# Score products of a differential attention: one mask product per bank ahead of four score products that alternate between two row groups

## Chip, core and metric

The kernel runs on one core of a Trainium2 chip. The metric is the device time of the program in microseconds (us), lower is better. Engines are named TensorE (PE; PEld is its weight load), VectorE (DVE), ScalarE (ACT), GpSimd (POOL) and SyncE (SP, which issues the DMAs here).

## What is computed

One layer of a streaming encoder for 256 tokens of width 2048. A conditioning vector gives shifts, scales and gates; one input projection feeds two groups of heads; an output projection and a gated feed-forward follow. Everything is in f32. One group, `mlstm`, has four heads of a matrix memory. The other, which the change concerns, is a differential attention: eight heads with two softmax maps each over 64 dimensions, and 128-wide values.

```python
def diff_attention(q, k, v, lam):
    # q,k (B,H,2,S,64): two maps; v (B,H,S,128)
    for j in range(S // 128):              # two blocks of 128 queries
        q0 = j * 128; kend = q0 + 128
        s = jnp.einsum('bhmqd,bhmkd->bhmqk', q[:, :, :, q0:kend], k[:, :, :, :kend]) * scale
        allowed = k_chunk[None, :] <= q_chunk[:, None]        # chunks of 64 tokens
        p = jax.nn.softmax(jnp.where(allowed, s, -jnp.inf), axis=-1)
        a = p[:, :, 0] - lam * p[:, :, 1]
        outs.append(jnp.einsum('bhqk,bhkd->bhqd', a, v[:, :, :kend]))
```

A head has four score blocks: query block 0 against 128 keys and query block 1 against 256 keys, for each of the two maps. In each, the last 128 key columns are the diagonal block, in which the first 64 queries may not see the last 64 keys.

## The kernel before

The main stream is a row of 392 "ticks". A tick multiplies 256 rows of a weight matrix, 512 columns wide, with all 256 tokens. Weights and activations are split into a high and a low part (`wh`, `wl` and for instance `hh`, `hl`), so a tick has twelve products of 128x512 into an accumulator `acc` (lines 568 to 570). A weight tile comes by DMA as `r`; ScalarE makes `wh` (line 211), VectorE makes `wl` (line 181). Three raw tiles and four pairs `wh`, `wl` may be alive, and SyncE issues the next load when one comes free.

All other work is written as generators. A planner (`Plan`) places their steps between halves of ticks by estimated costs of each engine and by free banks: four PSUM banks of 128x512 (`misc`, `BANKS = 4`) are shared by this work. The resulting order is fixed when the program is built, and each engine works through its own queue. Among this work are the modulation (`gv`: four products of 128x256 in the four 32-column groups of the array, from tiles `ada`) and the attention.

`attend(h)` handles a head. It takes two banks, `sc[0]` and `sc[1]`, one for each map. The two maps of a head lie on partitions 0 to 63 and 64 to 127 of `qT` and `kT`, so a map's score product uses 64 rows of the array, the lower or the upper ones. The mask is added by a bf16 product of an identity (`identb`) with a mask tile (`bmask`), which uses the whole array. Then VectorE finds negative row maxima (`st`, line 196), POOL scales them, ScalarE takes exp with a sum (`pm`, line 211), which frees the banks, VectorE combines the maps, and TensorE transposes the result (`aT`). `attend_values` multiplies with the values (`po`), and `finish_attention` makes the parts `odh` and `odl` for the output projection. A wait between engines goes by whole tiles: the first maximum of a bank waits for the last product that writes the bank.

Of the kernel before, what the change touches and what calls it, by code (L numbers as in the profile page):

```python
# [12 lines left out]
BF16 = mybir.dt.bfloat16  # L13
# [5 lines left out]
P = 128  # L19
D = 2048  # L20
NEG = -1.0e30
# [57 lines left out]


class Work:
    """Background work in steps; a step follows the one before it by at least a tick."""

    def __init__(self, name, gen, after):
        self.name, self.gen, self.after = name, gen, after
# [2 lines left out]


class Plan:  # L90
    """Interleaves the steps of background work with the ticks of the main matrix products."""

    def __init__(self):
        self.now = 0
# [70 lines left out]
def tile_block(ctx, tc, x, c, pos, par, w_ada, w_in, w_gt, w_out, w_gu, w_dn, out):  # L165
    nc = tc.nc
# [6 lines left out]
    ctx.enter_context(tc.manual_schedule())  # L173
    plan = Plan()

# [1 line left out]
    def fs(ap):  # L177
        return math.prod(ap.shape[1:])

# [15 lines left out]
    def red(o, a, op, negate=False):  # L195
        nc.vector.tensor_reduce(o, a, axis=AX.X, op=op, negate=negate)
        plan.v += fs(a) / 960 + 0.07

    def rec(o, a):
        nc.vector.reciprocal(o, a)  # L200
        plan.v += fs(o) / 120 + 0.07
# [13 lines left out]
    def mm(o, l, r, start, stop, passes=4, **kw):  # L215
        nc.tensor.matmul(o, l, r, start=start, stop=stop, **kw)  # L216
        plan.p += passes * max(fs(r), 64) / 2400

    def tr(o, a):
        nc.tensor.transpose(o, a, ident[:])  # L220
        plan.p += 0.06

    def slab(name, dt=F32):
        return sl.tile([P, 1024], dt, name=name, tag="slab")

    def misc(name):
        return psM.tile([P, 512], F32, name=name, tag="misc")

    def const(shape, name, dt=F32):
        return cp.tile(shape, dt, name=name)  # L230

    def tok(t, i):
        return t[:, i * 512:(i + 1) * 512]

# [1 line left out]
    part = const([P, NPAR - 256], "part")  # L236
    nc.sync.dma_start(part[:], par[:, :NPAR - 256])

    def par_(name):
        o, w = OFF[name]  # L240
        return part[:, o:o + w]
# [14 lines left out]
    for cb in range(4):  # L256
        load_x(cb)

# [1 line left out]
    ones = const([P, P], "ones")  # L260
    nc.gpsimd.memset(ones[:], 1.0)
    ident = const([P, P], "ident")
# [1 line left out]
    identb = const([P, P], "identb", BF16)  # L264
# [9 lines left out]
    for i in range(2):  # L274
# [8 lines left out]
    nc.gpsimd.memset(cmask[:], 0.0)  # L283
    nc.gpsimd.affine_select(out=cmask[:], in_=cmask[:], pattern=[[-1, P]], compare_op=ALU.is_ge,
                            fill=NEG, base=0, channel_multiplier=1)
    bmask = const([P, P], "bmask", BF16)
    nc.gpsimd.memset(bmask[:], 0.0)
    nc.gpsimd.memset(bmask[0:64, 64:128], NEG)
    junk = const([P, 512], "junk", BF16)

    act(scol[:, :, 0], par_("cc"), AF.Silu)
# [3 lines left out]
        mm(pq[:], ones[0:1, :], crow[0:1, q * 512:(q + 1) * 512], True, True)  # L295
        act(tok(silc[q // 2], q % 2), pq[:], AF.Silu)

# [1 line left out]
    items = []  # L299
    for s, t in ((1, 0), (4, 3)):  # L300
        for p in range(8):
# [172 lines left out]
        act(hi[:, q], full, AF.Copy)  # L474
        tt(lo[:, q], full, hi[:, q].bitcast(F32), ALU.subtract)

# [1 line left out]
    ticks = []  # L478

    def visit(accname, first, last, acts, src, name, halves, ready=(), done=None):  # L480
        """halves: list of (kb, half) in the order of K; acts(kb) gives (hi, lo)."""
        for n, (kb, h) in enumerate(halves):
            ticks.append(dict(acc=accname, start=first and n == 0, stop=last and n == len(halves) - 1,
                              act=acts, kb=kb, h=h, src=src, name=name, ready=ready,
                              done=done if n == len(halves) - 1 else None, split=None, mid=None))
# [60 lines left out]
    apart = {}  # L546

    def acc_tile(acc, k):
        """The accumulator of token tile k; those that are drained one by one have tiles of their own."""
        if acc in apart and k == 1:  # L550
            return apart[acc][:]
        return tok(accs[acc], k)
# [17 lines left out]
        nc.tensor.matmul(o, al[:, s], wh[:, r], start=False, stop=t["stop"] and j == 1)  # L570

    def products(i, half):
        """Half of a tick; the two ticks that end a group with "split" go token tile by token tile."""
        t = ticks[i]
        if t["split"] is None:
            for k in range(2):
                product(i, half, k)
        else:
            first = i - t["split"]
            for j in range(2):  # L580
                product(first + half, j, t["split"])
        if half == 1 and t["split"] != 0:
            for n in range(i - (t["split"] or 0), i + 1):
                del wtiles[n]

# [1 line left out]
    ropet = {}  # L587
    wqk = const([P, 1], "wqk")
    lam = const([P, 4], "lam")
# [67 lines left out]
        ts(lam[:, 2:3], lam[:, 2:3], -LAM0, None, ALU.add)  # L657
        ts(subc[:], par_("sub"), 1.0 - LAM0, None, ALU.mult)

# [1 line left out]
    proj = {}  # L661
    gwt = const([P, 16, 16], "gwt", F32R)
    gts = early[:, 768:1024]
    small = slab("small")
# [25 lines left out]
            tt(gts[0:16, :], gts[0:16, :], pg[0:16, 0:256], ALU.add)  # L690
        plan.rel(1)

# [1 line left out]
    sclq = const([P, 2, 16], "sclq")  # L694
    rstk = const([P, 2, 16], "rstk")
    qT, kT = {}, {}
# [55 lines left out]
    def attend(h):  # L752
        g, hh = divmod(h, 4)
        yield 2
        sc = [misc(f"sc{h}_{m}") for m in range(2)]
        blocks = []
        for t in range(2):
            ke = 128 * (t + 1)
            for m in range(2):
                pr = slice(m * 64, m * 64 + 64)  # L760
                o = sc[m][:, t * 128:t * 128 + ke]
                mm(o, qT[g][pr, hh * 256 + t * 128:hh * 256 + t * 128 + 128], kT[g][pr, hh * 256:hh * 256 + ke],
                   True, False)
                mm(o[:, t * 128:], identb[:], bmask[:], False, True, passes=1)
                blocks.append((t, m, o))
        yield 0
        st = sm.tile([P, 2, 8], F32, name=f"st{h}", tag="st", bufs=4)
        for t, m, o in blocks:
            red(st[:, t, m:m + 1], o, ALU.max, negate=True)
        scale = sclq[:, :, h * 2:h * 2 + 2]  # L770
        nc.gpsimd.tensor_tensor(st[:, :, 2:4], st[:, :, 0:2], scale, op=ALU.mult)
        yield 0
        work = slab(f"pm{h}")
        pm = {}
        for t, m, o in blocks:
            ke = 128 * (t + 1)
            a = ((640, 512), (0, 256))[t][m]
            pm[t, m] = work[:, a:a + ke]
            act(pm[t, m], o, AF.Exp, bias=st[:, t, 2 + m:3 + m], scale=scale[:, t, m:m + 1],
                accum=rs0[g][:, hh, t:t + 1] if m == 0 else st[:, t, 4:5])  # L780
        plan.rel(2)
        yield 0
        rec(st[:, :, 5], st[:, :, 4])
        stt(st[:, :, 6], rs0[g][:, hh], lam[:, 2:3], st[:, :, 5], ALU.mult, ALU.mult)
        for t in range(2):
            stt(pm[t, 0], pm[t, 1], st[:, t, 6:7], pm[t, 0], ALU.mult, ALU.add)
        yield 1
        pa = misc(f"aT{h}")
        for t in range(2):
            for s in range(t + 1):  # L790
                tr(pa[:, (t + s) * 128:(t + s + 1) * 128], pm[t, 0][:, s * 128:(s + 1) * 128])
        yield 0
        if h // 2 not in aTs:
            aTs[h // 2] = slab(f"aTs{h // 2}")
        act(aTs[h // 2][:, (h % 2) * 384:(h % 2) * 384 + 384], pa[:, :384], AF.Copy)
        plan.rel(1)
# [45 lines left out]
        plan.rel(2)  # L842
        mixT[2 + g] = (hi, lo)

# [1 line left out]
    cw = par_("cw").rearrange("p (t j) -> p t j", t=8)  # L846
    cbias = par_("cb")
    mT = {}
# [173 lines left out]
        plan.rel(2)  # L1022
        mixT[pair] = (hi, lo)

# [1 line left out]
    def gate_rows(s, rows, name):  # L1026
        yield 0
        modcol(s, 0, 16)
# [37 lines left out]
        return go  # L1066

    def turn(stage, heads):
        """The last products of w_out and the first of w_gate_up go token tile by token tile; this is what lies between."""
        if stage == 0:  # L1070
            residual_half(("wo", 3), rows1, 3, xs[3], 0)
            square_x(1, 3, 0, SQ0)
            finish_rms(1, 0)
            for p in range(2):
                next(heads[p, 0])
        elif stage == 1:
            plan.free -= 2
            for p in range(2):
                next(heads[p, 0])
        elif stage == 2:  # L1080
            residual_half(("wo", 3), rows1, 3, xs[3], 1)
            del accs["wo", 3], apart["wo", 3]
            plan.rel(1)
            next(heads[0, 0], None)
            square_x(1, 3, 1, SQ1)
            next(heads[1, 0], None)
            finish_rms(1, 1)
            for p in range(2):
                next(heads[p, 1])
        elif stage == 3:  # L1090
            plan.free -= 2
            for p in range(2):
                next(heads[p, 1])
        else:
            for p in range(2):
                next(heads[p, 1], None)
            plan.mark("norm2")
# [2 lines left out]
        yield 0  # L1100
        act(junk[:, 0:1], epst[:, 0:1], AF.Sqrt)

# [1 line left out]
    fpart = {}  # L1104
    aT = {}
    out_v = out.rearrange("(t p) (c n) -> c p t n", p=P, n=512)
# [70 lines left out]
        for k in range(2):  # L1177
            ticks[k - 2].update(split=k, mid=fn(k), done=None)

# [1 line left out]
    spans = {}  # L1181

    def pairs(p0, p1):
# [6 lines left out]
    for n, (groups, p0, p1) in enumerate(SWEEPS):  # L1190
        a = len(ticks)
# [4 lines left out]
    a = len(ticks)  # L1196
# [13 lines left out]
    for r, (p0, p1) in enumerate(FSWEEPS):  # L1210
        a = len(ticks)
# [10 lines left out]
    a = len(ticks)  # L1222
# [4 lines left out]
    a = len(ticks)  # L1227
# [6 lines left out]
    spans["dn"] = (a, len(ticks))  # L1234
    group_chunks()

    # how many quarters of w_ada each span of ticks takes: (first tick, last tick, items)
    loads = []

    def load(span, n, margin):  # L1240
# [9 lines left out]
            n += k * min(max(i + 1 - a, 0), b - a) / (b - a)  # L1250
        return min(int(n + 1e-6), len(items))

# [1 line left out]
    plan.t = 3.2  # L1254
    ada_dma(4)
    weights_dma(1)
# [70 lines left out]
        plan.add(f"h1_{p}", make_hT(1, p), [f"ada4_{p}", f"ada3_{p}", "norm2"])  # L1327
    plan.add("rows2", gate_rows(5, rows2, "g2r"), [f"ada5_{p}" for p in range(8)] + ["aT10"])

# [1 line left out]
    pending = []  # L1331
    turning = spans["wo"][1]
    heads = {(p, k): make_h2T(p, k) for p in range(2) for k in range(2)}
# [44 lines left out]


class Lazy:  # L1380
    """A generator that is made when its first step runs; that step needs no bank before it."""

    def __init__(self, fn, *args):
        self.fn, self.args, self.gen, self.asked = fn, args, None, False
# [82 lines left out]
```

## Time and profile before

| | us |
|---|---|
| median of 3 runs | 1253.47 (1249.21 to 1253.92) |
| profiled execution: span, first to last instruction | 1246.5 |
| profiled execution: its own time | not given; only the span is |
| PE busy in the span | 1224.0 (98%) |
| DVE, ACT, POOL busy | 815.9, 587.4, 112.2 |
| mean granted TensorE clock | 0.993 |

The profile shows one execution. A row of a timeline has start, duration, engine, line of the code, operation, output and inputs, shapes and a count; rows of the same kind that follow each other are merged. Matmuls overlap in the array, so TensorE's busy time says little, and distances between starts are what counts. The chain is the work that ended last, followed back from the end: what lies on it sets the time. An f32 score product is recorded as two passes, each with a weight load.

### The profile page before, as it was taken

How to read it: one execution, taken by the hardware profiler on the slowest of the kernel's cores; microseconds unless marked ns; L12 is line 12 of the kernel's file. 1: busy time of each engine (PE TensorE's matmuls, PEld its weight loads, DVE VectorE, ACT ScalarE, POOL GpSimd, SP SyncE). 2: the span in 40 equal slices, each digit the busy share in tenths (PEclk: the TensorE clock that was granted, in tenths of full speed). 3: DMA queues.
4: the chain of work that ended last, by engine and by line, in shares of the span. 5: the costliest groups of instructions: out<-in, count | busy, mean ns of one | idle time of the engine just before them, and what ended most of it. 6: DMA issues, size and time to landing. Idle time of an engine off the chain costs nothing.

```text
span 1246.5 us, 15450 instructions
## 1 busy us (share of the span) xinstructions
PE 1224.0 (98%) x5858; PEld 963.2 (77%) x5858; DVE 815.9 (65%) x1064; ACT 587.4 (47%) x817; POOL 112.2 (9%) x249
## 2 busy tenths in 40 slices
PE   6999999999999999999999999999999999999998
PEld 2667877667778788788888888888888878888886
DVE  2657976557667998777988986555445454545453
ACT  3654444446646644765434454434344443434332
POOL 1010221200302412011100000000000000000000
PEclk9999999989999999999999999999999999999999
DMA  8889997746755989698998856555555545646461
GB/s 332 300 299 349 343 377 282 281 151 249 256 219 194 330 331 353 264 341 302 354 352 332 309 181 218 201 176 200 188 183 197 183 169 195 220 169 223 165 251 54
DMA packets 63260, 313.84 MB, mean 252 GB/s; under 512 B 6993, under 2 KB 7377, under 8 KB 41169
## 3 DMA queue, kind: packets, MB, share of 16 engines
q1 hardware_dynamic: 63186, 312.86, 69.1%
q8 instruction: 46, 0.75, 0.2%
q14 instruction: 28, 0.23, 0.1%
HBM read 310.73 MB, written 2.10 MB: 251 GB/s over the span
## 4 chain that ended last, share of the span: by engine, by line
PE 95%; DMA 2%; DVE 1%; ACT 1%; issue 0%; SPq 0%; POOL 0%; ACTq 0%
PE gv L216 3%; PE sc L216 2%; DMA ada<-in_w_ada_dram 2%; PE acc('dn', 0)_8051 L570 2%; PE acc('dn', 0)_8051 L568 2%; PE acc('dn', 2)_8853 L570 2%; PE acc('dn', 2)_8853 L569 2%; PE acc('dn', 1)_8473 L570 2%; PE acc('dn', 1)_8473 L569 2%; PE acc('dn', 0)_8051 L569 2%; PE acc('dn', 2)_8853 L568 2%; PE acc('dn', 1)_8473 L568 2%; PE apart('dn', 3)_9234 L570 1%; PE apart('dn', 3)_9234 L569 1%; PE acc('dn', 3)_9233 L570 1%; PE acc('dn', 3)_9233 L569 1%
## 5 line engine op out<-in xcount | busy, mean ns | idle before, releaser
L181 DVE TENSOR_TENSOR wl<-r,wh 128x1024 fp32r<-128x1024 f32 x392 | 474.4, 1222 | 252.0 <-ACT wh L211 250.6
L211 ACT ACTIVATE wh<-r 128x1024 fp32r<-128x1024 f32 x392 | 410.3, 1058 | 414.6 <-DMA r<-in_w_gu_dram 64.7
L185 DVE SCALAR_TENSOR_TENSOR ada<-ada,silc 128x1024 f32<-128x1024 f32 x120 | 144.7, 1218 | 0.0
L376 POOL TENSOR_TENSOR modc<-part,gsum 128x2 f32<-128x2 f32 (+1 forms) x34 | 24.5, 722 | 396.5 <-DVE ada L185 277.7
L216 PE MATMUL gv<-ada,early 128*32 128x256 f32 x576 | 47.1, 420 | 4.6 <-DMA ada<-in_w_ada_dram 4.4
L216 PEld LDWEIGHTS gv<-ada,early 128*32 128x32 f32 x576 | 13.3, 112 | 30.5 <-issue 20.7
L568 PE MATMUL acc('dn', 0)_8051<-wh,aTh 128*128 128x512 f32 x88 | 35.9, 408 | 0.0
L378 POOL TENSOR_TENSOR modc<-modc,gsum 128x2 f32<-128x2 f32 (+1 forms) x58 | 30.9, 533 | 46.8 <-DVE ada L185 43.4
L570 PE MATMUL acc('dn', 0)_8051<-wh,aTl 128*128 128x512 f32 x88 | 34.3, 390 | 0.0
L569 PE MATMUL acc('dn', 0)_8051<-wl,aTh 128*128 128x512 f32 x88 | 34.3, 389 | 0.0
L568 PE MATMUL acc('dn', 1)_8473<-wh,aTh 128*128 128x512 f32 x88 | 34.2, 389 | 0.0
L569 PE MATMUL acc('dn', 1)_8473<-wl,aTh 128*128 128x512 f32 x88 | 34.2, 389 | 0.0
L570 PE MATMUL acc('dn', 1)_8473<-wh,aTl 128*128 128x512 f32 x88 | 34.2, 389 | 0.0
L568 PE MATMUL acc('dn', 2)_8853<-wh,aTh 128*128 128x512 f32 x88 | 34.2, 389 | 0.0
L569 PE MATMUL acc('dn', 2)_8853<-wl,aTh 128*128 128x512 f32 x88 | 34.2, 389 | 0.0
L570 PE MATMUL acc('dn', 2)_8853<-wh,aTl 128*128 128x512 f32 x88 | 34.2, 389 | 0.0
L181 DVE TENSOR_TENSOR hl<-hx,hh 128x512 fp32r<-128x512 f32 (+1 forms) x18 | 11.4, 632 | 26.7 <-ACT hh L211 26.6
L211 ACT ACTIVATE hx<-pt,modc,gcol 128x256 f32<-128x256 f32 (+1 forms) x36 | 17.4, 534 | 16.8 <-PE pt L220 11.7
L211 ACT ACTIVATE gr<-gv 128x256 f32<-128x256 f32 x18 | 6.9, 383 | 34.5 <-PE gv L216 34.5
L216 PE MATMUL sc<-kT,qT 64*128 64x128 f32 (+1 forms) x64 | 20.2, 397 | 0.0
L211 ACT ACTIVATE aTh<-at 128x512 fp32r<-128x512 f32 x22 | 11.9, 595 | 17.2 <-PE at L220 17.2
L569 PEld LDWEIGHTS acc('dn', 0)_8051<-wl,aTh 128*128 128x128 f32 x88 | 16.5, 188 | 4.2 <-issue 1.0
(987 smaller groups left out, 3041.6 us busy)
## 6 DMA issues: line engine op xcount, KB each, us to landing
ada<-in_w_ada_dram SPq DMA_DIRECT2D x192, 512.0 KB, 5.6
r<-in_w_gu_dram SPq DMA_DIRECT2D x76, 1024.0 KB, 5.1
r<-in_w_dn_dram SPq DMA_DIRECT2D x44, 1024.0 KB, 4.8
r<-in_w_in_dram SPq DMA_DIRECT2D x36, 1024.0 KB, 7.1
r<-in_w_out_dram SPq DMA_DIRECT2D x16, 1024.0 KB, 7.4
r<-in_w_in_dram SPq DMA_DIRECT2D x24, 512.0 KB, 5.9
r<-in_w_gu_dram SPq DMA_DIRECT2D x24, 512.0 KB, 5.2
x<-in_x_dram SPq DMA_DIRECT2D x4, 512.0 KB, 5.8
```

Of the source, the lines that this page charges most:

```text
L181: nc.vector.tensor_tensor(o, a, b, op=op)
L185: nc.vector.scalar_tensor_tensor(out=o, in0=a, scalar=s, in1=b, op0=op0, op1=op1, accum_out=accum)
L211: nc.scalar.activation(o, a, func, **kw)
L216: nc.tensor.matmul(o, l, r, start=start, stop=stop, **kw)
L376: nc.gpsimd.tensor_tensor(o, parts[0], parts[1], op=ALU.add)
L378: nc.gpsimd.tensor_tensor(o, o, y, op=ALU.add)
L568: nc.tensor.matmul(o, ah[:, s], wh[:, r], start=t["start"] and j == 0, stop=False)
L569: nc.tensor.matmul(o, ah[:, s], wl[:, r], start=False, stop=False)
L570: nc.tensor.matmul(o, al[:, s], wh[:, r], start=False, stop=t["stop"] and j == 1)
```

## The change

The mask tile becomes two copies side by side, 256 columns. For a head, first one mask product goes to each bank, over columns 128 to 383, and opens the accumulation of the bank. Then come four score products: the 256-key block of map 0 and of map 1 into columns 0 to 255, then the 128-key block of map 0 and of map 1 into columns 256 to 383. They add to the mask where there is one and otherwise write. Before, the order was block by block, each score followed by its mask. The planner is told of two passes for a score instead of four.

```diff
-    bmask = const([P, P], "bmask", BF16)
+    bmask = const([P, 2 * P], "bmask", BF16)
     nc.gpsimd.memset(bmask[:], 0.0)
-    nc.gpsimd.memset(bmask[0:64, 64:128], NEG)
+    for y in range(2):
+        nc.gpsimd.memset(bmask[0:64, y * P + 64:y * P + 128], NEG)
...
         blocks = []
-        for t in range(2):
+        for m in range(2):
+            mm(sc[m][:, 128:384], identb[:], bmask[:], True, False, passes=1, skip_group_check=True)
+        for t, off in ((1, 0), (0, 256)):
             ke = 128 * (t + 1)
             for m in range(2):
                 pr = slice(m * 64, m * 64 + 64)
-                o = sc[m][:, t * 128:t * 128 + ke]
+                o = sc[m][:, off:off + ke]
                 mm(o, qT[g][pr, hh * 256 + t * 128:hh * 256 + t * 128 + 128], kT[g][pr, hh * 256:hh * 256 + ke],
-                   True, False)
-                mm(o[:, t * 128:], identb[:], bmask[:], False, True, passes=1)
+                   False, True, passes=2, skip_group_check=True)
                 blocks.append((t, m, o))
```

The rest of the diff takes out comments. The order of the work around the heads stays as it was, on every engine.

TensorE's queue at head 0, before. A product's name has the bank with its map (`sc_0` is map 0), the inputs, and the size of the output; an f32 product loads its weights itself:

```order
L570 MATMUL acc('in', 7, 4)_2233<-wh_2149,hl_2_1195 128x512
L216 MATMUL sc_0_2242<-kT_2230,qT_2057 128x128
L216 LDWEIGHTS identb
L216 MATMUL sc_0_2242<-bmask,identb 128x128
L216 MATMUL sc_1_2243<-kT_2230,qT_2057 128x128
L216 LDWEIGHTS identb
L216 MATMUL sc_1_2243<-bmask,identb 128x128
L216 MATMUL sc_0_2242<-kT_2230,qT_2057 128x256
L216 LDWEIGHTS identb
L216 MATMUL sc_0_2242<-bmask,identb 128x128
L216 MATMUL sc_1_2243<-kT_2230,qT_2057 128x256
L216 LDWEIGHTS identb
```

The same place in the changed kernel, up to the next product of the main stream:

```order
L571 MATMUL acc('in', 7, 4)_2234<-wh_2150,hl_2_1196 128x512
L216 LDWEIGHTS identb
L216 MATMUL sc_0_2243<-bmask,identb 128x256
L216 LDWEIGHTS identb
L216 MATMUL sc_1_2244<-bmask,identb 128x256
L216 MATMUL sc_0_2243<-kT_2231,qT_2058 128x256
L216 MATMUL sc_1_2244<-kT_2231,qT_2058 128x256
L216 MATMUL sc_0_2243<-kT_2231,qT_2058 128x128
L216 MATMUL sc_1_2244<-kT_2231,qT_2058 128x128
L569 MATMUL acc('in', 7, 4)_2234<-wh_2150,hh_2_1195 128x512
```

Scores of the two maps now stand next to each other, where a mask stood between them, and a head has two masks in place of four. ScalarE's queue for the exps of head 0, before and then in the changed kernel (`pm` is the result, `rs` and `st` hold the sums):

```order
L211 ACTIVATE gr_2_2280<-gv_2_2158 128x256
L211 ACT_TABLE_LOAD
L211 ACTIVATE pm_2282,rs_0_147<-sc_0_2242,st_2260,sclq 128x128
L211 ACTIVATE pm_2282,st_2260<-sc_1_2243,st_2260,sclq 128x128
L211 ACTIVATE pm_2282,rs_0_147<-sc_0_2242,st_2260,sclq 128x256
L211 ACTIVATE pm_2282,st_2260<-sc_1_2243,st_2260,sclq 128x256
L211 ACTIVATE wh_2293<-r_2151 128x1024
```

```order
L211 ACTIVATE gr_2_2279<-gv_2_2159 128x256
L211 ACT_TABLE_LOAD
L211 ACTIVATE pm_2281,rs_0_148<-sc_0_2243,st_2259,sclq 128x256
L211 ACTIVATE pm_2281,st_2259<-sc_1_2244,st_2259,sclq 128x256
L211 ACTIVATE pm_2281,rs_0_148<-sc_0_2243,st_2259,sclq 128x128
L211 ACTIVATE pm_2281,st_2259<-sc_1_2244,st_2259,sclq 128x128
L211 ACTIVATE wh_2292<-r_2152 128x1024
```

The 256-wide exps come first now; the bank of map 0 is still freed by the third and that of map 1 by the fourth.

## Prediction

> **What bounds the kernel now.** I read the page's busy shares and chain first, to see which engine sets the end. Then the chain piece by piece between 250 and 385 us, where the scores are computed.
>
> ```profile
> span 1246.5 us, 15450 instructions
> PE 1224.0 (98%) x5858; PEld 963.2 (77%) x5858; DVE 815.9 (65%) x1064; ACT 587.4 (47%) x817; POOL 112.2 (9%) x249
> PE 95%; DMA 2%; DVE 1%; ACT 1%; issue 0%; SPq 0%; POOL 0%; ACTq 0%
> ...
> 254.40 2.73 PE sc L216 x12
> 262.10 6.93 PE sc L216 x24
> 280.57 2.73 PE sc L216 x12
> ...
> 352.71 2.73 PE sc L216 x12
> 361.57 5.46 PE sc L216 x24
> 381.30 2.73 PE sc L216 x12
> ```
>
> TensorE is the chain for 95% of the span, and the score products (`sc`) of all eight heads lie on it: four heads alone at 2.73 us each, and two pairs issued back to back at 6.93 and 5.46 us. So the question is what a head costs TensorE, and whether the time won there reaches the end. TensorE's own rows around head 0 (start, duration; an x2 row is the two passes of one f32 product):
>
> ```profile
> 254.01 0.39 PE L570 MATMUL acc('in', 7, 4)_2233<-wh,hl 128*128 128x512 f32 x1
> 254.33 0.48 PE L216 MATMUL sc<-kT,qT 64*128 64x128 f32 x2
> 254.75 0.10 PEld L216 LDWEIGHTS <-identb 128*128 128x128 bf16 x1
> 254.75 0.23 PE L216 MATMUL sc<-bmask,identb 128*128 128x128 bf16 x1
> 254.91 0.49 PE L216 MATMUL sc<-kT,qT 64*128 64x128 f32 x2
> 255.33 0.23 PE L216 MATMUL sc<-bmask,identb 128*128 128x128 bf16 x1
> 255.49 0.70 PE L216 MATMUL sc<-kT,qT 64*128 64x256 f32 x2
> 256.11 0.23 PE L216 MATMUL sc<-bmask,identb 128*128 128x128 bf16 x1
> 256.27 0.70 PE L216 MATMUL sc<-kT,qT 64*128 64x256 f32 x2
> 256.90 0.23 PE L216 MATMUL sc<-bmask,identb 128*128 128x128 bf16 x1
> 256.94 0.47 PE L568 MATMUL acc('in', 7, 4)_2233<-wh,hh 128*128 128x512 f32 x1
> 257.25 0.39 PE L569 MATMUL acc('in', 7, 4)_2233<-wl,hh 128*128 128x512 f32 x1
> 257.48 0.40 PE L570 MATMUL acc('in', 7, 4)_2233<-wh,hl 128*128 128x512 f32 x1
> ```
>
> Durations overlap, so only distances between starts count. A regular product of the main stream follows after 0.23 (257.25 to 257.48). From 254.01 to 257.25 pass 3.24 us, where two regular steps would take 0.46: **a head costs 2.78 us**, 22.2 for eight. A 256-column score holds TensorE for 0.62 (255.49 to 256.11), a 128-column one for 0.42 (254.33 to 254.75). A mask is followed by a full-array product after 0.04 (256.90 to 256.94), but by a 64-row score after 0.16 (254.75 to 254.91): changing between whole array and row groups costs about 0.12.
>
> **Part 1: the masks.** Four masks of 128 columns become two of 256. Last `acc` to first mask: a regular 0.23, both use the whole array. Mask to mask lies between 0.08 (twice the 0.04) and 0.23; the order still shows a weight load before each, whose row reads 0.10, so I take 0.11. Second mask to first score: 0.16 and 0.04 for the doubled columns, 0.20.
>
> **Part 2: the scores.** No row before shows products of the two row groups next to each other: a mask always stands between. The nearest are the modulation products, four neighbours in four column groups:
>
> ```profile
> 258.50 0.64 PE L216 MATMUL gv<-ada,early 128*32 128x256 f32 x8
> 259.07 0.50 PE L568 MATMUL acc('in', 7, 4)_2233<-wh,hh 128*128 128x512 f32 x1
> ...
> 258.50 0.42 PE L216 MATMUL gv<-ada,early 128*32 128x256 f32 x4
> ```
>
> Eight passes of 256 columns, four products, take 0.57 in all (258.50 to 259.07), less than the two passes of one 256-column score with the change behind it (0.62). So neighbours in different parts of the array run side by side there. Taken over to row groups, a map's score hides the other map's: 0.62 + 0.42 less one change of 0.12, since only the last leaves the row groups, is 0.92. If they ran one after another without a change in between: 2(0.62 + 0.42) - 3 x 0.12 = 1.72; with a change at each, 2.08. I take 0.92, because the `gv` row is nearest in form (f32, neighbours that share no part of the array), and keep the other two as the far end.
>
> Sum for a head: 0.23 + 0.11 + 0.20 + 0.92 and the unchanged 0.31 of the following `acc` (256.94 to 257.25), less 0.46, is 1.31. Against 2.78 that saves 1.47, **11.8 us for eight heads**.
>
> [...]
>
> **Part 3: the clock.** One stretch of scores made TensorE slow. The columns are window, width, busy time of PE, PEld, DVE, ACT and POOL, then the granted clock, DMA share and GB/s:
>
> ```profile
> 262.00:265.40 3.40, 3.40 (x17) 2.01 (x16) 2.25 (x6) 2.94 (x6) 0.00 (x0) 1.00 0.78 318
> 265.45:272.20 6.75, 6.75 (x17) 4.33 (x18) 4.39 (x13) 2.08 (x8) 1.32 (x2) 0.50 0.05 6
> ...
> 268.80 0.78 PE L568 MATMUL acc('in', 7, 4)_2233<-wh,hh 128*128 128x512 f32 x1
> 269.37 0.63 PE L569 MATMUL acc('in', 7, 4)_2233<-wl,hh 128*128 128x512 f32 x1
> 272.55 0.40 PE L568 MATMUL acc('in', 7, 4)_2233<-wh,hh 128*128 128x512 f32 x1
> ```
>
> After 3.4 us of nothing but scores the clock fell to 0.50 for about 6.8 us. The pair took 6.93 instead of 5.46 (1.47 lost), and nine steps of `acc` took 3.75 (268.80 to 272.55) instead of 0.31 + 8 x 0.23 = 2.15 (1.60 lost): 3.1 us. A lone head (2.73) never did this. By the sum above a pair will last about as long as a lone head now, so the drop should go: **3.1 us**. Bounds: 0, if the runs behind the median had none, and 6.2, if both pairs had one. I take one, as the trace shows.
>
> [...]
>
> **Part 4: costs set at nothing.** TensorE could stall for four things.
>
> ```profile
> PE acc('wo', 0)_3650 L570 <- DVE odl L185: 0.7, 1, 0.7
> ...
> 406.56 0.25 PE acc('in', 11, 6)_3545 L570
> 406.83 0.04 DVE proj L181
> 416.06 0.68 DVE odl L185
> ...
> 262.39 0.56 ACT L211 ACTIVATE pm<-sc,st,sclq 128x256 f32<-128x256 f32 x1
> 264.76 0.48 PE L216 MATMUL sc<-kT,qT 64*128 64x128 f32 x2
> ...
> 3.72 0.20 POOL L287 MEMSET bmask<- 128x128 bf16 x1
> 3.98 0.14 POOL L288 MEMSET bmask<- 64x64 bf16 x1
> 24.10 0.19 POOL L376 TENSOR_TENSOR modc<-part,gsum 128x2 f32<-128x2 f32 x1 [19.97 <-ACT gsum L211]
> ```
>
> The first row is the only wait of TensorE between 240 and 440 us: weights come in time, and a TensorE that is 15 us earlier frees their buffers earlier too. That one wait ends a chain on VectorE which TensorE itself starts (406.56 to 406.83), so it moves along; 0 to 1 us. Next, the second head of a pair takes its banks from the head before the pair, whose last exp ends at 262.95, while TensorE comes at 264.76. Half of the room goes: head 0's saving moves exp and scores alike, but head 1's 1.47 moves only the scores, and the second mask comes 0.11 after the first, so 264.76 - 1.47 + 0.11 = 263.40 against 262.95. It still fits; 0 to 0.5 a pair. Reductions and exps are the same in number and shape, in another order, wide ones first. On POOL a memset doubles and one is added, some 0.3 us; POOL then idles until 24.10, and the first mask stands at 254.75.
>
> The sum is 11.8 + 3.1 = 14.9: the profiled execution would have a span of 1231.6. The data give its span, not its own time; the median of the runs, 1253.47, lies 7.0 above it, so I carry the saving over: 1238.6, rounded up to **1239** for part 4.
>
> **The rivals.** [...]
> (b) Row groups run one after another: 1.72, 0.67 a head, 5.4. A pair still lasts over 4 us, so I credit half of the clock: 1246.5. For it: the only row of row groups shows none side by side.
> (c) The change does hardly what it says: each switch of row group drains as a mask does now (2.08), 0.31 a head, 2.5, and the clock falls as before: 1251.0. Against it: the order keeps the group size, only the group changes.
> (d) Slower: at each switch of row group weight loads come into the open.
>
> ```profile
> L216 PEld LDWEIGHTS sc<-kT,qT x64: 182/186/335, 254.3 to 383.3; 64*128 64x128 f32 x64
> ```
>
> The row gives the scores' weight loads, least, median and longest in ns. Eight at 0.19 on top of 2.08 are 3.6; a head then costs 3.99, 1.21 more, and the kernel 1263. It decides as soon as a head's four scores take over 2.39. Against it: the `gv` group of 0.57 has eight loads in it.
>
> **Chances.** My forecast 0.58, (a) 0.12, (b) 0.14, (c) 0.11, (d) 0.05. A measurement of this kernel tells about 0.5% (6.3 us) from no change: the runs before spread over 4.7 us. The forecast, (a) and half of (b), which lies at that border, are faster: 0.77 and a little for two clock drops, 0.79. (c) and the rest of (b) make the same 0.16, (d) the slower 0.05. The range runs from 1234 (two drops gone, mask step at its low end) to 1248 (b without the clock); outside are (c), (d) and a little.
>
> **What would show it.** [...] In the chain eight `sc` pieces of some 1.2 us, pairs 2.5. Granted clock 1.00 all through 250 to 390. One wait of about 0.7 at `odl`, as before; a new one at the second mask of a pair, or growing waits on VectorE after 410, would eat the gain. I am wrong if row groups don't run side by side in f32, or if the median runs had no clock drop.

## The result and the profile after

| | changed kernel | kernel before, beside it |
|---|---|---|
| median of the runs | 1234.02 us (1233.24 to 1235.92, 4 runs) | 1253.38 us (1249.21 to 1253.92, 4 runs) |
| ratio | 0.9858, 95% interval 0.9840 to 0.9876 | |
| span of the profiled execution | 1231.5 us | 1246.5 us |
| granted clock, mean over the span | 0.992 | 0.993 |

The change makes the kernel 19.4 us faster. Forecast were 14.4 us (1239, from 1253.4), with a range that begins at 1234. Medians and comparisons here and below leave out two runs that took far longer than all others, one of 3107 us of the changed kernel and one of 1541 us of the kernel whose pairs the planner broke up.

First the page of the changed kernel: span, busy shares, shares of the chain.

```profile
span 1231.5 us, 15419 instructions
PE 1208.9 (98%) x5842; PEld 956.2 (78%) x5842; DVE 815.3 (66%) x1064; ACT 587.1 (48%) x817; POOL 113.2 (9%) x250
PE 96%; DMA 1%; DVE 1%; ACT 1%; issue 0%; SPq 0%; POOL 0%; ACTq 0%
```

TensorE is still the bound: its busy time fell by 15.1 us (1224.0 to 1208.9) and the span by 15.0. The chain of waits of the changed kernel, its `sc` pieces (start, length, count of passes):

```profile
254.40 1.09 PE sc L216 x10
...
260.61 2.27 PE sc L216 x20
...
273.25 1.09 PE sc L216 x10
...
343.88 1.09 PE sc L216 x10
...
351.24 2.27 PE sc L216 x20
...
367.92 1.07 PE sc L216 x10
```

Lone heads went from 2.73 to 1.09 and pairs from 6.93 and 5.46 to 2.27. TensorE's rows around head 0, from the last `acc` step ahead of it to the third behind it, and below them the same score group in a stretch that ends at 254.57, then, with the second mask ahead of it, in one that reaches to 254.70:

```profile
254.01 0.39 PE L571 MATMUL acc('in', 7, 4)_2234<-wh,hl 128*128 128x512 f32 x1
254.25 0.39 PE L216 MATMUL sc<-bmask,identb 128*128 128x256 bf16 x2
254.57 0.92 PE L216 MATMUL sc<-kT,qT 64*128 64x256 f32 x8
255.42 0.50 PE L569 MATMUL acc('in', 7, 4)_2234<-wh,hh 128*128 128x512 f32 x1
255.75 0.40 PE L570 MATMUL acc('in', 7, 4)_2234<-wl,hh 128*128 128x512 f32 x1
255.99 0.40 PE L571 MATMUL acc('in', 7, 4)_2234<-wh,hl 128*128 128x512 f32 x1
...
254.57 0.48 PE L216 MATMUL sc<-kT,qT 64*128 64x256 f32 x1
...
254.36 0.27 PE L216 MATMUL sc<-bmask,identb 128*128 128x256 bf16 x1
254.57 0.49 PE L216 MATMUL sc<-kT,qT 64*128 64x256 f32 x2
```

Between the two `acc` steps at 254.01 and 255.75 pass 1.74 us (3.24 before); less the two regular steps of 0.46 a head costs 1.28, against 2.78. Eight passes of scores stand in 0.85 (254.57 to 255.42). The last `sc` rows, of one pass (0.48) and of two (0.49), show why: a second pass begins within 0.13 us of the first and ends only 0.01 after it, though one pass takes 0.48. By the single records it starts 6 ns after it. It is taken to be map 1's: in the kernel before, where a mask stands between the maps, no two score passes begin less than 0.21 us apart. The two row groups run side by side from the first pass on.

Granted clock and the waits of TensorE (the stretch from 250 to 390 us, columns as in the prediction, and the waits from 240 to 440):

```profile
250.00:390.00 140.00, 140.00 (x838) 105.50 (x838) 105.32 (x219) 88.15 (x218) 24.56 (x68) 1.00 0.66 235
...
PE acc('wo', 0)_3635 L571 <- DVE odl L185: 0.7, 1, 0.7
```

The clock stays at 1.00, TensorE is busy for all 140 us, and the one wait is the one of before, as long as before. The saving is not given back. Against the profile of before, the same steps of the main stream start 7.6 us earlier at 273 us (three heads, 4.5, and the clock drop, 3.0), 10.4 earlier at 355, 14.9 earlier at 384, and 14.9 to 15.0 earlier up to the end.

This leaves two questions. The spans differ by 15.0 as forecast (14.9), but the medians by 19.4: where are the other 4 us? And which part of the edit saves the 1.50 of a head: masks taken out from between, masks widened, row groups side by side, or the alternation of maps?

### The profile page after: what moved, and what is told of

Read it like the earlier page. It is cut to its first block, busy times and chain, and to the rows that moved or that the text cites. A ratio compares the mean times of both kernels' runs of the same rounds, so it can differ in the third digit from the quotient of the medians.

```text
span 1231.5 us, 15419 instructions
## 1 busy us (share of the span) xinstructions
PE 1208.9 (98%) x5842; PEld 956.2 (78%) x5842; DVE 815.3 (66%) x1064; ACT 587.1 (48%) x817; POOL 113.2 (9%) x250
## 4 chain that ended last, share of the span: by engine, by line
PE 96%; DMA 1%; DVE 1%; ACT 1%; issue 0%; SPq 0%; POOL 0%; ACTq 0%
PE gv L216 3%; PE acc('dn', 0)_8036 L571 2%; PE acc('dn', 0)_8036 L569 2%; PE acc('dn', 2)_8838 L571 2%; PE acc('dn', 2)_8838 L570 2%; PE acc('dn', 1)_8458 L571 2%; PE acc('dn', 1)_8458 L570 2%; PE acc('dn', 0)_8036 L570 2%; PE acc('dn', 1)_8458 L569 2%; PE acc('dn', 2)_8838 L569 2%; DMA ada<-in_w_ada_dram 1%; PE apart('dn', 3)_9219 L571 1%; PE apart('dn', 3)_9219 L570 1%; PE acc('dn', 3)_9218 L571 1%; PE acc('dn', 3)_9218 L570 1%; PE apart('dn', 3)_9219 L569 1%
## 5 line engine op out<-in xcount | busy, mean ns | idle before, releaser
L569 PE MATMUL acc('dn', 0)_8036<-wh,aTh 128*128 128x512 f32 x88 | 35.9, 408 | 0.0
L571 PE MATMUL acc('dn', 0)_8036<-wh,aTl 128*128 128x512 f32 x88 | 34.3, 390 | 0.0
L570 PE MATMUL acc('dn', 0)_8036<-wl,aTh 128*128 128x512 f32 x88 | 34.3, 389 | 0.0
L569 PE MATMUL acc('dn', 1)_8458<-wh,aTh 128*128 128x512 f32 x88 | 34.2, 389 | 0.0
L570 PE MATMUL acc('dn', 1)_8458<-wl,aTh 128*128 128x512 f32 x88 | 34.2, 389 | 0.0
L571 PE MATMUL acc('dn', 1)_8458<-wh,aTl 128*128 128x512 f32 x88 | 34.2, 389 | 0.0
L569 PE MATMUL acc('dn', 2)_8838<-wh,aTh 128*128 128x512 f32 x88 | 34.2, 389 | 0.0
L570 PE MATMUL acc('dn', 2)_8838<-wl,aTh 128*128 128x512 f32 x88 | 34.2, 389 | 0.0
L571 PE MATMUL acc('dn', 2)_8838<-wh,aTl 128*128 128x512 f32 x88 | 34.2, 389 | 0.0
L570 PEld LDWEIGHTS acc('dn', 0)_8036<-wl,aTh 128*128 128x128 f32 x88 | 16.5, 188 | 4.2 <-issue 1.0
```

The costliest lines, as they stand in the source:

```text
L569: nc.tensor.matmul(o, ah[:, s], wh[:, r], start=t["start"] and j == 0, stop=False)
L570: nc.tensor.matmul(o, ah[:, s], wl[:, r], start=False, stop=False)
```

## Experiments

### The kernel before once more: what its runs lose to the clock

The kernel before, unchanged, 12 runs.

> The kernel before, unchanged, for the span and clock of each run. The change saved 15.0 us of span (1246.5 to 1231.5) but 19.4 us of the median, so 4.4 us are open. Theory (clock): the profiled execution had one clock drop in the scores and the median run has more, so runs near 1253 show a lower mean clock than 0.993, and a profile of one shows two drops of TensorE between 250 and 370 us, or a longer one. Rival (other): mean clocks of the runs are alike, about 0.993, and the profile shows the 4 us in waits for a DMA or another engine.

Median 1251.07, ratio 1.0002 (0.9982 to 1.0022). The runs lie in two groups with nothing between: six from 1247.2 to 1249.2, six from 1253.0 to 1254.7. (Of all 63 runs of this kernel on record, two lie between the groups, at 1250.7 and 1251.2.) The profiled execution took 1253.44 with a span of 1251.7. Its clock in three stretches, and the two pairs in its chain:

```profile
266.70:273.40 6.70, 6.70 (x17) 4.32 (x17) 3.80 (x11) 2.08 (x8) 1.32 (x2) 0.50 0.17 32
365.70:372.40 6.70, 6.70 (x17) 4.21 (x17) 1.51 (x5) 0.00 (x0) 0.41 (x2) 0.50 0.36 146
509.10:512.30 3.20, 3.20 (x9) 2.52 (x9) 2.56 (x8) 1.66 (x3) 0.00 (x0) 0.50 0.01 5
...
262.69 6.52 PE sc L216 x24
...
362.24 6.88 PE sc L216 x24
```

Here both pairs fall to 0.50, and a third, shorter drop stands at 509 us. Against the profile of the first section this execution is 0.6 late up to 355 us, 3.7 behind the second pair, and 5.3 behind the drop at 509, which makes the 5.2 between the spans (1251.7 and 1246.5). Run time is 1.7 above span here (1253.44 - 1251.7), and also for the changed kernel (1233.24 - 1231.5). So the execution with a span of 1246.5, on which the prediction was built, stands for a run of some 1248.2: it is of the lower group, and the median it was compared with is of the upper one. Other drops, at the start (ahead of 75 us), vary from run to run too (the first profile has 1.00 from 36.75 to 265.40; here steps of `acc` at 69.92 and 70.35 take 0.43 instead of 0.23), so the mean clock of a run does not sort the two groups, though that had been expected.

Short stretches show where the granted clock changes, here at both ends of the first pair's drop:

```profile
266.60:266.64 0.04, 0.04 (x1) 0.04 (x2) 0.04 (x1) 0.00 (x0) 0.00 (x0) 1.00 0.00 0
266.66:266.70 0.04, 0.04 (x1) 0.04 (x2) 0.04 (x2) 0.00 (x0) 0.00 (x0) 0.50 0.00 0
...
273.43:273.46 0.03, 0.03 (x2) 0.03 (x1) 0.00 (x0) 0.00 (x0) 0.00 (x0) 0.50 0.00 0
273.48:273.52 0.04, 0.04 (x2) 0.04 (x1) 0.00 (x0) 0.00 (x0) 0.00 (x0) 1.00 0.48 205
```

This drop begins at 266.65 and lasts 6.82; the other two fill the stretches above, 6.70 and 3.20 us, or more. In the profile of the first section, the first pair's drop and the stretches of the second pair, which kept its clock:

```profile
265.42:272.25 6.83, 6.83 (x17) 4.41 (x18) 4.47 (x14) 2.08 (x8) 1.32 (x2) 0.50 0.08 10
...
361.00:364.40 3.40, 3.40 (x16) 1.88 (x15) 2.53 (x7) 2.21 (x4) 0.00 (x0) 1.00 0.40 143
364.40:367.80 3.40, 3.40 (x16) 2.16 (x17) 1.92 (x7) 0.00 (x0) 0.20 (x1) 1.00 0.88 304
```

From a pair's first score to the drop pass 3.3 us there (262.10 to 265.42), 4.0 here in the first pair (262.69 to 266.65) and at most 3.5 in the second (362.24 to 365.70). The pair that kept its clock, from 361.57 to 367.03 in the first profile, is longer than all of these, at 5.46. What decides which pairs of a run lose their clock, no run shows.

### The kernel before, with the pairs broken up by the planner

No two heads' scores are issued within one step any more (the line of the planner that picks the next work):

```diff
+            if w.name.startswith("at") and w.need == 2:
+                if self.scored + 2 > self.now:
+                    continue
+                self.scored = self.now
```

> The kernel before with one edit: two heads' scores never stand back to back, so the two pairs of 5.4 us are gone, and the products themselves are as before. Clock theory: no stretch of nothing but scores is longer than 2.7 us, the clock stays at 1.00 between 250 and 390 us, and the median falls by what the change gained beyond its 12.0 us of products: 19.4 - 12.0 = 7.4, to 1246. Rival (one drop only): 3.1 us, to 1250.3. Rival (other): no change, 1253. A head's cost in the profile stays 2.78 us.

It missed: 1259.52 (1258.1 to 1260.35, 5 runs), ratio 1.0071 (1.0048 to 1.0093). No drop is left between 250 and 390, but the heads that now come later hold up the end of the attention. TensorE's waits of this kernel from 395 to 430 us, and the clock from 415 us:

```profile
PE ot L225 <- DVE o L186: 7.2, 1, 7.2
PE acc('wo', 0)_3611 L575 <- DVE odl L190: 1.0, 1, 1.0
...
415.00:425.00 10.00, 6.49 (x19) 4.43 (x20) 8.75 (x13) 2.81 (x4) 4.63 (x11) 0.50 0.76 278
```

TensorE stands for 7.2 us, until 417.5, and the granted clock reads 0.50 over the stretch from 415 to 425, which begins within the wait. The experiment moved more than the one thing, so it says nothing on what the pairs' drops cost. The next one does it without moving any work.

### The kernel before, with full-array work inside each pair

Eight f32 products over the whole array, into a bank that the scores then overwrite, ahead of the second head of each pair:

```diff
         sc = [misc(f"sc{h}_{m}") for m in range(2)]
         blocks = []
+        for n in range(8 if h in (2, 6) else 0):
+            nc.tensor.matmul(sc[0][:, 0:128], ident[:], ones[:], start=True, stop=True)
```

> The kernel before, with eight whole-array f32 products of 128x128 put between the two heads of each of the two pairs (their result is overwritten): 1.7 us of full array splits each 5.4 us stretch into two of 2.7. Work added: 2 x 1.7 = 3.4 us. Clock theory: no drop between 250 and 390 us in the profile, the span without any drop is 1246.5 - 3.1 + 3.4 = 1246.8 and the time 1248.5, up to 1.6 more where the clock drops at about 509 us; the two clusters of before (about 1248 and 1253.5) become one. Rival (the gap has another cause): 3.4 us on top of before, two clusters at 1251 and 1257.

Median 1249.75 (1248.52 to 1252.97, 12 runs) against 1253.2 for the kernel before beside it (22 runs), ratio 0.9985 (0.9972 to 0.9998). Its chain at the first pair, the clock in two stretches, and the waits of TensorE from 480 to 520 us:

```profile
263.18 2.73 PE sc L216 x12
265.91 1.84 PE sc L758 x16
267.75 2.73 PE sc L216 x12
...
250.00:390.00 140.00, 140.00 (x806) 101.95 (x803) 93.48 (x195) 79.79 (x192) 21.51 (x63) 1.00 0.61 217
507.00:510.20 3.20, 3.20 (x9) 2.53 (x9) 2.56 (x8) 1.76 (x4) 0.00 (x0) 0.50 0.05 20
...
PE acc('gu', 0, 0)_4472 L568 <- ACT hh L211: 2.3, 2, 1.1
PE pt L220 <- DVE hx L190: 0.7, 1, 0.7
```

TensorE has 2 x 1.84 = 3.7 us more to do on its path, and yet the kernel is not slower: both pairs run at full clock now, and each half of a pair takes the 2.73 of a lone head. It is 1.9 us faster by the ratio (0.3 to 3.5) and 3.45 by the medians. The two differ because the runs of both kernels lie in groups: here seven from 1248.5 to 1249.9 and five from 1251.1 to 1253.0, where one group had been expected. By the ratio, the pairs' drops cost a run of the kernel before 1.9 + 3.7 = 5.6 us on average (4.0 to 7.2); two drops of 3.0 to 3.1 would be 6.1.

The drop near 507 remains in this profile. It stands behind waits of TensorE at the start of the feed-forward, 0.7 us for `pt` and 1.1 for the first half of `gu`, which begins at 506.45. The profile of the first section has waits of 2.3 and 0.7 there too, and no drop (1.00 from 272.30 to 1245.00), so the waits by themselves do not bring it. What does, no run shows.

### Scores and masks three times: is it the length of the stretch?

The changed kernel, each head's masks and scores computed three times (the last ones are used):

```diff
-        for m in range(2):
-            mm(sc[m][:, 128:384], identb[:], bmask[:], True, False, passes=1, skip_group_check=True)
-        for t, off in ((1, 0), (0, 256)):
...
+        for again in range(3):
+            for m in range(2):
+                mm(sc[m][:, 128:384], identb[:], bmask[:], True, False, passes=1, skip_group_check=True)
+            for t, off in ((1, 0), (0, 256)):
...
```

> The change with a head's masks and scores issued three times over (the last time counts): a pair lasts 7.1 us and a lone head 3.5 us, side by side throughout. Work added: 16 x 1.18 = 18.8 us, to 1252.8. Theory A (an array half empty drops the clock): the clock stays at 1.00 between 250 and 410 us, and the runs stay within 3 us, around 1253. Theory B (any stretch of scores longer than 3.4 us drops it): both pairs are over 6.8 us, so each run has at least two drops, each of 3 us or more: 1259 or above.

Median 1252.94 (1251.69 to 1254.65, 10 runs), ratio 1.001 (0.9994 to 1.0026). Its pieces in the chain and its clock:

```profile
255.40 3.44 PE sc L216 x30
...
263.98 6.98 PE sc L216 x60
...
250.00:390.00 140.00, 140.00 (x898) 102.98 (x895) 91.59 (x193) 77.05 (x180) 20.78 (x62) 1.00 0.60 216
```

A head is 2.35 longer (3.44 and 1.09), eight are 18.8, and 1234.1 + 18.8 = 1252.9 is what was measured: nothing is lost to the clock. A stretch of scores longer than the pairs of before, 6.98 us, leaves it at 1.00 when both row groups are at work. So the length alone is not the cause. What goes with the drop, which comes 3.3 to 4.0 us after a pair's first score, is a stretch in which each of nearly all products fills only one row group, half of the array, though TensorE is never idle by the profile. What in such a stretch counts is open: the empty half, or the changes between whole array and row groups, of which a head has eight in 2.73 us before and six in 3.44 here.

### Both maps in the same row group: what side by side is worth

The changed kernel; both maps read map 0's 64 rows of queries and keys, so map 1's scores are left out.

```diff
             for m in range(2):
-                pr = slice(m * 64, m * 64 + 64)
+                pr = slice(0, 64)
```

> The change, but the score products of map 1 read the rows of map 0 (so map 1's scores are left out, and map 0's stand in their place): all four products of a head use the same 64 rows of the array, so they cannot run side by side, and no mask stands between them. Theory (side by side): the four scores take about 1.7 us to the next acc instead of 0.86, 0.85 a head and 6.8 us in all more than the change, 1241; and since a pair is then over 4 us with half of the array empty, some runs drop the clock as before, up to 1246. Rival (masks): the changes at the masks were the cost, and one group is as quick as two: 1234.

Median 1240.24 (1239.42 to 1241.98), ratio 0.9910 (0.9882 to 0.9938). TensorE's rows at head 0, the first pair in the chain, and the clock:

```profile
255.22 0.39 PE L216 MATMUL sc<-bmask,identb 128*128 128x256 bf16 x2
255.54 1.57 PE L216 MATMUL sc<-kT,qT 64*128 64x256 f32 x8
257.04 0.50 PE L569 MATMUL acc('in', 7, 4)_2234<-wh,hh 128*128 128x512 f32 x1
...
262.26 3.56 PE sc L216 x20
...
250.00:390.00 140.00, 140.00 (x813) 106.20 (x810) 100.50 (x209) 86.53 (x212) 23.05 (x64) 1.00 0.64 231
```

The four scores take 1.50 (255.54 to 257.04) in place of 0.85. So of the 1.50 that a head saves, 0.65 come from the row groups side by side (5.2 us for eight) and the other 0.85 from masks that no longer stand between the scores (6.8 us). The second would be had without any overlap. The span is 6.2 longer than the changed kernel's (1237.7 and 1231.5); the 1.0 beyond the 5.2 lies ahead of head 0, whose first piece in the chain begins at 255.38 instead of 254.40.

The drop of the clock that was expected in some runs did not show: no run is above 1242, and the profile keeps 1.00. This does not separate the empty half of the array from the changes between whole array and row groups, because a pair ends after 3.56 us here, within the 3.3 to 4.0 us that passed ahead of the drops in the kernel before.

### Map by map: is it the alternation?

The changed kernel with both scores of map 0 first, then both of map 1:

```diff
-        for t, off in ((1, 0), (0, 256)):
-            ke = 128 * (t + 1)
-            for m in range(2):
+        for m in range(2):
+            for t, off in ((1, 0), (0, 256)):
+                ke = 128 * (t + 1)
```

> The change without the alternation: two wide masks first, then both scores of map 0, then both of map 1. Theory (side by side): the four scores take about 1.72 us up to the next acc in place of the 0.86 measured for the change, a head costs some 2.1 us, and the gain from the products is 8 x 0.7 = 5.4 us; a pair lasts over 4 us, so the clock can still drop. Median 1243 to 1249. Rival (masks): taking the masks from between the scores is the whole gain, alternation does nothing; the four scores take about 0.9 us and the time is that of the change, 1234.

The expected loss did not come: 1234.5 (1234.05 to 1234.69), ratio 0.9871 (0.9843 to 0.9899), as the changed kernel. TensorE's rows at head 0, and the forms of the score passes that begin up to 255.4 (least, median and longest in ns):

```profile
254.88 0.93 PE L216 MATMUL sc<-kT,qT 64*128 64x256 f32 x8
255.74 0.50 PE L569 MATMUL acc('in', 7, 4)_2234<-wh,hh 128*128 128x512 f32 x1
...
L216 PE MATMUL sc<-kT,qT x4: 376/428/480, 254.9 to 255.2; 64*128 64x256 f32 x4
```

The scores take 0.86. In program order map 0's two passes of 256 columns are followed by its two of 128 columns, and only then by map 1's. TensorE's queue, as the kernel builds it, has this order too. On the chip the first four passes are all 256 wide, so two of them are map 1's. The second begins within 0.12 us of the first, at 254.88, and is taken to be the other map's, since two passes of one product begin 0.21 us apart or more in the kernel before. So a product got ahead of one that stands before it in the program. Whether TensorE lets it pass, or a later step of compiling has put it there, no run here shows. Either way the order in which the code names the maps is not what gives the 0.65.

### Four masks of 128 first: is it the width?

The changed kernel, with the old masks, all four ahead of the scores:

```diff
-            mm(sc[m][:, 128:384], identb[:], bmask[:], True, False, passes=1, skip_group_check=True)
+            for y in range(2):
+                mm(sc[m][:, 128 + y * 128:256 + y * 128], identb[:], bmask[:, 0:128], y == 0, False, passes=1,
+                   skip_group_check=True)
```

> The change with four masks of 128 columns, as before in size, but all of them first: what the wider masks are worth by themselves. Theory: four whole-array bf16 products of 128 columns with a weight load each follow each other at the 0.11 of the load, so masks take 3 x 0.11 + 0.16 = 0.49 instead of 0.12 + 0.20 = 0.32: 0.17 a head, 1.4 us in all, 1235.5. Rival: no difference, 1234.1, if streaming the columns sets their pace.

No cost: 1234.68 (1233.4 to 1234.89), ratio 0.9873 (0.9849 to 0.9897). TensorE's rows at head 0:

```profile
254.40 0.40 PE L216 MATMUL sc<-bmask,identb 128*128 128x128 bf16 x4
254.73 0.92 PE L216 MATMUL sc<-kT,qT 64*128 64x256 f32 x8
```

Four narrow masks take 0.33 up to the first score, two wide ones 0.32. Narrow masks follow each other after 0.06 (three distances in 0.40 less the 0.23 that one mask lasts in the kernel before), less than the 0.10 of a weight load, and wide ones after 0.12 by the single records of the changed kernel, so the pace goes by the columns. The masks' gain comes from where they stand, not from their number or width.

### A mask inside the row groups

The nearest version that could be better: a mask as a product over one row of 64 (ones for the early queries by the mask's value for the late keys), so that masks also run in the row groups, side by side and without the change from the whole array.

```diff
+    early_q = const([P, P], "early_q", BF16)
+    nc.gpsimd.memset(early_q[:], 0.0)
     for y in range(2):
-        nc.gpsimd.memset(bmask[0:64, y * P + 64:y * P + 128], NEG)
+        nc.gpsimd.memset(early_q[y * 64:y * 64 + 1, 0:64], 1.0)
+        for z in range(2):
+            nc.gpsimd.memset(bmask[y * 64:y * 64 + 1, z * P + 64:z * P + 128], NEG)
...
-            mm(sc[m][:, 128:384], identb[:], bmask[:], True, False, passes=1, skip_group_check=True)
+            pr = slice(m * 64, m * 64 + 64)
+            mm(sc[m][:, 128:384], early_q[pr, :], bmask[pr, :], True, False, passes=1, skip_group_check=True)
```

> The change, with the mask product itself in the row groups: a 64-row product of one nonzero row each (early queries times late keys), one for each map, so that masks run side by side and a head changes once into row groups and once out, with no whole-array product between. Theory: last acc to first mask 0.32 instead of 0.23, masks side by side 0.11 instead of 0.119 + 0.203 = 0.32, the rest the same: 0.12 us a head less, 1.0 us in all, 1233.0. Rival: the change into row groups is not what costs 0.1 behind a mask; the time is that of the change, 1234.0, or a little more.

Median 1232.75 (1231.23 to 1235.10), ratio 0.9860 (0.9837 to 0.9883). The same kernel again, with the changed kernel beside it:

> The masks in the row groups once more, beside the changed kernel in the same call, since their gap is smaller than the spread of the kernel before. From its first profile a head costs 0.87 + 0.32 + 0.34 - 0.46 = 1.07 us instead of 1.28 and the whole stands 1.1 us ahead after the last head (one bank wait of 0.3 takes some of it): 1.1 us under the changed kernel's median, 1233.0. Rival: a drop of the clock or a wait elsewhere takes it back; equal medians.

Median 1233.33 (1231.74 to 1234.06), ratio 0.9862 (0.9841 to 0.9882).

> The changed kernel, unchanged, for more runs on the chip of these experiments. Theory: one cluster, 1233 to 1236; no drop in the scores in any run; what spread there is comes from a drop at about 490 us, 1.6 us in those runs that have it.

> The changed kernel again, for the comparison with the masks in the row groups: 1234.1.

The changed kernel took 1234.14 (1233.99 to 1234.68, ratio 0.9858, 0.9835 to 0.9881) and 1234.69 (1233.13 to 1235.23, 3 runs, ratio 0.9870, 0.9845 to 0.9894). TensorE's rows of the second kernel with masks in row groups, at head 0 and at the second head of the first pair:

```profile
253.98 0.39 PE L575 MATMUL acc('in', 7, 4)_2240<-wh,hl 128*128 128x512 f32 x1
254.30 0.28 PE L216 MATMUL sc<-bmask,early_q 64*128 64x256 bf16 x2
254.42 0.82 PE L216 MATMUL sc<-kT,qT 64*128 64x256 f32 x8
255.17 0.50 PE L573 MATMUL acc('in', 7, 4)_2240<-wh,hh 128*128 128x512 f32 x1
...
261.05 0.57 PE L216 MATMUL sc<-bmask,early_q 64*128 64x256 bf16 x2
261.36 0.92 PE L216 MATMUL sc<-kT,qT 64*128 64x256 f32 x8
```

From the last `acc` step to the next pass 1.19 (253.98 to 255.17), where the changed kernel has 1.41 (254.01 to 255.42): 0.22 a head, 1.8 for eight. In the pair some of it goes: the two masks lie within 0.28 at head 0 and within 0.57 here, since the second waits for its bank, whose last exp ends its read at 261.30 on ScalarE. That is the wait which the prediction had bounded by 0 to 0.5 a pair; in the changed kernel it is not there. All ten runs have a median of 1233.0, twelve of the changed kernel 1234.1. The 1.1 us between them, 0.1%, lies within the ratio intervals, so that this version is better is likely by the trace, and not shown by the times.

## Why the prediction was right, and where it was off

**What bounds the kernel** held: TensorE's busy time, the chain and the span fell together, by 15.

**Part 1, the masks.** Forecast 0.23, 0.11 and 0.20; measured 0.23, 0.12 and 0.20 (starts of the last `acc`, the two masks and the first score). The sizes were right, though the 0.11 was taken from the duration of a weight load and met the 0.12 by luck: narrow masks follow each other after 0.06. The reading behind them was too generous to the edit: fewer and wider masks are worth nothing (0.33 for four), only their place is.

**Part 2, the scores.** Forecast 0.92 side by side; measured 0.85. A head saves 1.50 instead of 1.47, eight save 12.0 instead of 11.8. Carrying the column groups' row over to row groups was right. The 0.12 that the chances give to (a) is for scores whose passes follow each other one by one in the order of the code. No run shows such an order: map 1's first pass stands 6 ns behind map 0's, and the map-by-map kernel begins with four passes of 256 columns, two of them map 1's. Rival (b)'s price, 1.72, was near: forced into one group the scores take 1.50. (c) and (d) did not occur; no start distance shows a drain or an open weight load between the maps (6 to 7 ns from a pass of one to that of the other).

**Part 3, the clock.** The mechanism held: a pair lost 3.0 to 3.1 us to a drop, and pairs of 2.27 us have none. The size failed, at the step "I take one, as the trace shows". The one profiled execution had one pair's drop; an execution near the median has both (6.1), and by the kernel with full-array work in its pairs the drops cost 5.6 us a run on average. The reason given, that a pair would last about as long as a lone head, is enough by itself, since the pieces of 2.73 in that kernel keep the clock. It is not the whole rule: 6.98 us of side-by-side scores keep it too, and the change brought that as well. The pairs that lost their clock had it at 0.50 within 3.3 to 4.0 us of their first score, and one of 5.46 us kept 1.00 throughout. What parts the two, and with them the two groups of runs, no run shows.

**Part 4, costs at nothing.** All were: no wait for a bank, `odl` 0.7 as before, no growth behind 384 us.

**From span to time.** The forecast span was 1231.6, the measured one 1231.5. The forecast time was 5.0 too high: 0.4 by rounding up to 1239, and 4.6 from "so I carry the saving over", where the 7.0 between the profiled span and the median were taken as a constant. Only 1.7 of them are, as the two kernels show whose profiled runs have a time. The other 5.3 are what the profiled run happened not to have, and the later profile of the kernel before shows them: 3.0 for the drop of the second pair, 1.6 for the drop at 509, and 0.6 at the start. The change takes the first away. The second is not in the profile of the changed kernel (1.00 from 72.35 to 1230 us), but that the change removes it is not shown by one profile.

The ledger from profile to profile: the kernel before at 1253.44 and the changed one at 1233.24 differ by 20.2, which is 12.0 for the heads, 6.1 for the drops of two pairs, 1.6 for the drop at 509 and 0.6 at the start. The medians differ by 19.4, mainly because the changed kernel's profiled run was 0.8 under its median.

That the range held the result (1234.02) is luck. Two drops gone and the mask step at its low end of 0.08 give 1253.5 - 11.8 - 6.2 - 0.2 = 1235.3; for the 1.3 us from there to the 1234 no term is given.

## What to carry over

In a kernel like this, products that fill only some row or column groups should stand next to each other, with whole-array work ahead of or behind them all: here a mask between two scores cost more (0.85 a head) than the lost overlap (0.65). Where the profiled execution's own time is not the median's, find out which drops or waits the median has before any difference between them is carried over as a constant. A run of TensorE without a gap is no proof of full clock: look at the granted clock behind long stretches that use part of the array (here 0.50 for 6.83 us, with TensorE busy all the while).

## What the runs showed of the hardware that was not expected

- Pairs that take 5.46 us at full clock, in which TensorE was busy throughout by the profile, but each of nearly all products filled only one 64-row group, had a granted clock of 0.50 from 3.3 to 4.0 us after their first score, for some 6.8 us (6.83 in the first profile), at a loss of 3.0 to 3.1 us each time. One such pair kept 1.00. Eight whole-array products (1.84 us) in the middle of such a pair kept it at 1.00, and 6.98 us with both row groups side by side kept it too.
- The stretches at 0.50 that begin and end within the span last 10.24 and 6.83 us in the first profile of the kernel before, and 13.65 and 3.41 in that of the changed kernel, all whole multiples of the shortest to 0.01.
- The kernel before has two groups of run times, 0.4% apart (of 63 runs 23 from 1246.8 to 1249.5 and 38 from 1252.3 to 1255.0), and a single profile shows one of them.
- With both scores of map 0 written first, the first four passes were all 256 columns wide, so two of map 1's began ahead of map 0's 128-column product, which is written before them.
- From the first of two whole-array masks to the first score pass 0.32 us, but only 0.12 when the masks are in the row groups (254.30 to 254.42). There the change from the whole array comes once, ahead of the masks (253.98 to 254.30 is 0.32, against a regular 0.23).
